# Hybrid attention block: sparse keys and values loaded in two halves, two silus moved behind the first query tiles, and the output projection's operands split two steps ahead

## The chip, the cores and the metric

The kernel runs on one core of a Trainium2 chip. The core has TensorE (PE in the profile) for matrix products, VectorE (DVE), ScalarE (ACT) and GpSimd (POOL) for elementwise work, and a queue (SP) from which most transfers are issued to 16 DMA engines. The metric is the device time of one execution in microseconds (us); smaller is better.

## The reference

One layer of a decoder with three head groups that read the same normalised input, 1024 positions of width 2048, all in float32:

```
h = rmsnorm(x, norm_g) @ w_in                    # one projection feeds everything
o_mla = mla_mixer(...) * silu(z_mla)             # 8 heads, latent attention, dense causal
o_nsa = nsa_mixer(...) * silu(z_nsa)             # 4 heads: compressed + selected + window branches
o_mem = memory_mixer(...) * silu(z_mem)          # 4 heads over 256 memory tokens
out = rmsnorm(x + concat(o_mla, o_nsa, o_mem) @ w_out, final_norm_g)
```

In the sparse (nsa) group each of 8 query tiles of 128 rows attends, per head, to 63 compressed blocks, to the selected keys `k_s, v_s` (here all earlier ones) and to a window of 512 of `k_w, v_w`.

## The kernel before

**Arithmetic.** Each float32 operand is split into a high and a low part (`split`: ACT writes the high part on line 118, DVE subtracts on line 112), and each product is three matmuls (`mm3`, lines 124 to 126). A 128x512 matmul then starts every 0.23 us.

**Buffers.** `big` (16 buffers of 128x2048), `slot` (8 of 128x1088), `wraw` (3) and `work` (4 of 128x1024 each) are pools; a tile waits until a buffer of its pool is free. PSUM has 8 banks: 4 `S`, 2 `T`, 2 `O`/`J`.

**Order.** There are three stages. In the input projection (to 1000 us of the profile) and in the output projection (from 1557 us) the instructions of PE, ACT, DVE and POOL keep the order in which the program writes them (`manual_schedule`); each engine executes its own in order. SP's queue, and everything in the attention stage between them, is ordered by a planner from its own estimates of durations. Every engine's queue, SP's too, is worked off in order: an instruction that waits holds up those behind it.

**Input projection.** Forty units `u` of 7 steps `s` each; a step is a product of 12 matmuls into one `S` bank, and `evac` takes it out. In the second half of the units `evac` adds the first half's sum from DRAM with an accumulating transfer from POOL's queue (lines 782 and 786). `post` finishes a unit; for the last unit it is two silus on ACT (line 795) and their stores, written after the last step. `at(u, s, ...)` hangs other work on a step: in the last unit `ul` the loads of the sparse group. `nsa_keys` loads the keys `ks` (4 `slot` tiles, which also get the compressed keys), `nsa_window` the window's keys (2 `big`), `nsa_aux` the causal mask of the compressed branch (`cmask`, `cm01`) and its values, `nsa_values_in` the values (2 `big`), and `nsa_masks` (line 1063) copies the masks on ACT.

**First query tiles.** For each head `h` and tile `i`, `nsa_scores` fills one to four `S` banks with scores, DVE adds the masks and takes the minimum (lines 1107 to 1114, and 1229 for the compressed branch with `cmask`), ACT takes the exponential (line 659) and so frees the bank, and after the reciprocal the weights are scaled (ACT line 1159, DVE and POOL line 1161), transposed, split and multiplied by the values. Tile `i` reads columns up to `128*(i+1)`, so tiles 0 to 3 need only the first 512 keys.

**Output projection.** 56 steps `t = 8p + k` of 24 matmuls (5.44 us), seven parts `p` of a fast matrix product. Step `t` multiplies the split attention output `ent[t]` (a `slot`) by the split weights `wsp[t]` (a `big`). `w_load`, `a_load` fetch them four steps ahead, `w_prep` splits the weights, `a_prep` first forms sums of attention outputs (part 2, 3 and 5) and then splits. After the last step of a part `oevac` takes all 8 banks out (lines 1612 to 1622). Beside it `oside` adds the residual, squares rows (line 1575), and in part 6 computes `inverse` (the row's 1/rms) and `scaled_out` of rows 0 to 3, on DVE (line 1595) or, with `on_act`, on ACT (line 1593). The last four steps' operands (52 to 55) are multiplied bank by bank at the end.

Of the kernel before, what the change touches and what calls it, by code (L numbers as in the profile page):

```python
# [52 lines left out]
def hybrid_block_kernel(ctx: ExitStack, tc, a, out):  # L53
# [734 lines left out]
    def post(u, n):  # L788
        p, uu = divmod(u, NU)
        o, j = outs[u][n], units[uu][n]  # L790
        if not p:
            V.tensor_tensor(o, o, mst["Rx"], op=ALU.mult)
            store(c0d[uu][:, n * 1024:(n + 1) * 1024], o)
        elif j >= T_ZMLA:
            S.activation(o, o, AF.Silu)
            store(zd[j - T_ZMLA], o)
        elif j < 8:
            store(cd[j], o)
            c_sum(j, o)
# [206 lines left out]
    at(ul, 0, lambda: nsa_keys())  # L1006
    at(ul, 1, lambda: nsa_window())
    at(ul, 3, lambda: nsa_aux())
    at(ul, 4, lambda: nsa_values_in())
    at(ul, 6, lambda: nsa_masks())  # L1010
# [13 lines left out]
    def nsa_window():  # L1024
        kw = big()
        nsa["kwm"] = (kw[:, :1024], kw[:, 1024:])
        load(f(kw), kwd)
        kw = big()
        kw1, kw2 = nsa["kw"] = kw[:, :1024], kw[:, 1024:]
        for r0 in (0, 64):  # L1030
            load(f(kw1[r0:r0 + 64]), kswh[64:])
        load(f(kw2[:64]), kswl[64:])
        load(f(kw2[64:]), posd[:, 64:])

    def nsa_values_in():
        nsa["vs"], nsa["vw"] = big(), big()
        load(f(nsa["vs"]), vsd)
        load(f(nsa["vw"]), vwd)

    def nsa_keys():  # L1040

        kh, kl, k1, k2 = [slot() for _ in range(4)]
        nsa["ks"] = (kh, kl), k1, k2
        load(f(kh[:, :64]), kcd[:, :64])
        load(f(kl[:, :64]), kcd[:, 64:128])
        load(f(k1[:, :64]), kcd[:, 128:192])
        load(f(k2[:64, :64]), kcd[:64, 192:])
        load(f(kh[:, 64:]), ksd[:, :1024])
        load(f(kl[:, 64:]), ksd[:, 1024:])
        for r0 in (0, 64):  # L1050
            load(f(k1[r0:r0 + 64, 64:]), kswh[:64])
        load(f(k2[:64, 64:]), kswl[:64])
        load(f(k2[64:]), posd)
# [26 lines left out]
    post(2 * NU - 1, 0)  # L1080
    post(2 * NU - 1, 1)
# [326 lines left out]
    for h in range(4):  # L1408
        q = qn
        for i in range(8):  # L1410
# [5 lines left out]
            src = nsa_scores(h, q, i)  # L1416
            if h == 3 and i == 7:
# [69 lines left out]
    def a_prep(t, dst=None):  # L1487
# [8 lines left out]
        if p == 2:  # L1496
            V.tensor_tensor(s1, r[0], r[1], op=ALU.add)
            V.tensor_tensor(s2, s1, r[2], op=ALU.subtract)
            src = s2
        elif p == 3:  # L1500
            V.tensor_tensor(r[0], r[0], r[1], op=ALU.subtract)
            src = r[0]
        elif p == 4:
            src = s1
        elif p == 5:
            V.tensor_tensor(s2, r[0], s2, op=ALU.subtract)
            src = s2
        else:
            src = r[0]
        e = slot()[:, :1024] if dst is None else dst  # L1510
        split(e[:, :512], e[:, 512:], src)
        ent[t] = e

    def o_first():

        e = big()
        for t in range(2):
# [3 lines left out]
            a_prep(t, e[:, t * 1024:t * 1024 + 1024])  # L1521
# [111 lines left out]
    def oside(p, k):  # L1633

        i = k // 2
        if p == 1 and k % 2 == 0:
            Y[i] = big(F32)
            load(Y[i][:, L_], a["x"][i * P:(i + 1) * P, L_])
        if p == 3 and k < 4:
# [12 lines left out]
        if p == 6:  # L1652
            if k < 4:
                square(Y[k][:, L_], st_(k, 0))
                square(Y[k][:, H_], st_(k, 1))
            if 0 < k <= 4:
                r = inverse(k - 1, 2)
                scaled_out(k - 1, r, L_)
# [6 lines left out]
    w_prep(2)  # L1665
    a_prep(2)
    for t in range(NT):
        p, k = divmod(t, 8)
        if t + 4 < NT:
            w_load(t + 4)  # L1670
            a_load(t + 4)
        if t + 3 < NT:
            w_prep(t + 3)
            a_prep(t + 3)
# [141 lines left out]
```

## Time and profile before

| | |
|---|---|
| median of 3 runs | 1892.62 us (1887.09 to 1897.51) |
| profiled execution | 1892.9 us, span 1891.1 us |
| PE busy | 1786.8 us (94% of the span) |
| DVE, ACT, POOL busy | 1317.0, 854.9, 323.8 us |
| DMA | 351.91 MB, mean 186 GB/s |
| mean granted clock of TensorE | 0.979 |

A row of the timeline gives start, duration, engine, line, operation, out<-in, shapes and, in brackets, the engine's idle time just before and what ended it. The granted clock is a share of full speed: 1.00 is 2.4 GHz, 0.50 is 1.2 GHz.

### The profile page before, as it was taken

The numbers are of one execution on the slowest core, as the hardware profiler recorded it, in microseconds if no ns is written. First come the engines' busy times: TensorE is split into PE (matmuls) and PEld (weight loads), VectorE is DVE, ScalarE is ACT, GpSimd is POOL, SyncE is SP. The second block draws the span as 40 slices with busy tenths as digits, with TensorE's granted clock in tenths as the row PEclk, the third lists the DMA queues.
The fourth block names the chain that finished last, engine by engine and source line by source line (L and its number), as shares of the span: only waits on it lengthen the run. The fifth ranks groups of instructions, "written<-read, shape, count | busy, mean of one in ns | idle before, by whom it ended". The sixth has DMA issues, their size and how long they took to land. (4 is left out here: it accounts for less than half of the span.)

```text
span 1891.1 us, 26430 instructions
## 1 busy us (share of the span) xinstructions
PE 1786.8 (94%) x9294; PEld 1523.0 (81%) x9294; DVE 1317.0 (70%) x2478; ACT 854.9 (45%) x1712; POOL 323.8 (17%) x433
## 2 busy tenths in 40 slices
PE   8999999999999999999997999999999999989996
PEld 7888878887777777877776898888998988877885
DVE  7976878976866655666564887868778783454777
ACT  8754222222434344544555665545455453222344
POOL 0002322323233313233231222200000000000020
PEclk9999999999999999999998999999999999999998
DMA  6554877786678657978998233432122144654564
GB/s 220 187 189 165 286 263 267 253 298 237 225 211 255 161 173 231 293 214 243 307 265 242 68 97 109 167 114 62 46 77 64 57 154 150 226 167 145 172 194 191
DMA packets 124930, 351.91 MB, mean 186 GB/s; under 512 B 15355, under 2 KB 39613, under 8 KB 121725
## 3 DMA queue, kind: packets, MB, share of 16 engines
q1 hardware_dynamic: 119037, 329.25, 51.7%
q0 software_dynamic: 5760, 20.97, 6.3%
q8 instruction: 73, 1.20, 0.3%
q14 instruction: 60, 0.49, 0.1%
HBM read 242.14 MB, written 108.02 MB: 185 GB/s over the span
## 5 line engine op out<-in xcount | busy, mean ns | idle before, releaser
L124 PE MATMUL S<-big,wh 128*128 128x512 f32 x1336 | 528.7, 396 | 25.2 <-DVE work L772 8.3
L125 PE MATMUL S<-big,wh 128*128 128x512 f32 x1336 | 525.7, 393 | 4.4 <-DVE big L112 4.4
L126 PE MATMUL S<-big,wh 128*128 128x512 f32 x1336 | 525.3, 393 | 1.3 <-DVE wh L112 1.2
L124 PEld LDWEIGHTS S<-big,wh 128*128 128x128 f32 x1336 | 254.0, 190 | 82.0 <-issue 12.5
L125 PEld LDWEIGHTS S<-big,wh 128*128 128x128 f32 x1336 | 254.3, 190 | 56.7 <-DVE big L112 5.9
L126 PEld LDWEIGHTS S<-big,wh 128*128 128x128 f32 x1336 | 253.6, 190 | 56.9 <-DVE wh L112 3.0
L112 DVE TENSOR_TENSOR wh<-wraw,wh 128x512 fp32r<-128x512 f32 (+2 forms) x226 | 199.0, 882 | 73.8 <-ACT wh L118 73.6
L118 ACT ACTIVATE wh<-wraw 128x512 fp32r<-128x512 f32 (+2 forms) x226 | 145.4, 659 | 90.4 <-PE S L126 44.2
L112 DVE TENSOR_TENSOR big<-wraw,big 128x1024 fp32r<-128x1024 f32 x56 | 73.9, 1320 | 105.1 <-ACT big L118 100.5
L733 POOL TENSOR_TENSOR wraw<-wraw 128x512 f32<-128x512 f32 x38 | 56.6, 1488 | 459.6 <-DMA wraw<-in_w_feat 394.6
L659 ACT ACTIVATE work<-S,st 128x512 f32<-128x512 f32 (+3 forms) x148 | 84.6, 573 | 86.5 <-DVE st L1114 35.1
L118 ACT ACTIVATE wh<-rs 128x512 fp32r<-128x512 f32 x80 | 50.2, 628 | 157.7 <-POOL rs L734 125.6
L112 DVE TENSOR_TENSOR wh<-rs,wh 128x512 fp32r<-128x512 f32 x80 | 63.0, 787 | 65.5 <-ACT wh L118 65.4
L118 ACT ACTIVATE big<-wraw 128x1024 fp32r<-128x1024 f32 x56 | 59.2, 1056 | 85.6 <-PE J L126 59.4
L124 PE MATMUL J<-big,wh 128*128 128x512 f32 x214 | 84.1, 393 | 0.8 <-ACT wh L118 0.7
L125 PE MATMUL J<-big,wh 128*128 128x512 f32 x214 | 84.0, 393 | 0.0
L126 PE MATMUL J<-big,wh 128*128 128x512 f32 x214 | 83.9, 392 | 0.0
L118 ACT ACTIVATE wh<-T 128x512 fp32r<-128x512 f32 (+2 forms) x112 | 53.0, 504 | 45.6 <-PE T L1179 29.5
L770 ACT ACTIVATE work<-S 128x512 f32<-128x512 f32 x40 | 23.9, 597 | 106.7 <-PE S L126 99.2
L112 DVE TENSOR_TENSOR wh<-T,wh 128x512 fp32r<-128x512 f32 (+2 forms) x112 | 61.5, 569 | 10.6 <-ACT wh L118 10.3
L1443 POOL MEMSET wh<- 128x128 f32 x64 | 13.8, 228 | 291.8 <-PE O L125 173.6
L1096 PE MATMUL S<-big,big 128*128 128x512 f32 (+2 forms) x144 | 52.9, 367 | 9.7 <-ACT wraw L659 9.7
(378 smaller groups left out, 4132.1 us busy)
## 6 DMA issues: line engine op xcount, KB each, us to landing
wraw<-in_w_feat SPq DMA_DIRECT2D x80, 512.0 KB, 5.5
part<-work SPq DMA_DIRECT2D x40, 512.0 KB, 3.7
work<-part POOLq DMA_DIRECT2D x40, 512.0 KB, 6.4
work<-og SPq DMA_DIRECT2D x72, 256.0 KB, 4.0
wh<-in_w_o SPq DMA_DIRECT2D x32, 512.0 KB, 7.2
t<-wh SPq DMA_DIRECT2D x32, 512.0 KB, 3.0
wraw<-t SPq DMA_DIRECT2D x32, 512.0 KB, 3.7
wraw<-in_w_o SPq DMA_DIRECT2D x24, 512.0 KB, 3.9
```

Source lines behind the costliest of these rows:

```text
L112: V.tensor_tensor(dst, src, f(hi), op=ALU.subtract)
L118: S.activation(hi, src, AF.Copy)
L124: PE.matmul(dst, sh, mh, start=start, stop=False, skip_group_check=shared)
L125: PE.matmul(dst, sh, ml, start=False, stop=False, skip_group_check=shared)
L126: PE.matmul(dst, sl, mh, start=False, stop=stop, skip_group_check=shared)
L659: S.activation(dst, src, AF.Exp, bias=m, scale=-1.0, accum_out=s)
L733: E.tensor_tensor(B12, B22, B12, op=ALU.subtract)
L770: S.activation(C21, B, AF.Copy)
L1096: PE.matmul(d, qm[0][:, c:c + P], km[0][:, k0:k0 + n], start=True, stop=False)
L1443: G.memset(f(t[:, o:o + P]), 0.0)
```

## The change

It has four pieces. (1) The keys, window keys and values of the sparse group are loaded in two halves of 512 columns; the first halves of keys and values and the masks' copy are written one step earlier than before, the masks' load three steps, the window's first half where it was; the second halves follow at step 5 of the last unit. (2) The two last silus move out of the input projection: they are written behind `nsa_scores` of tiles 1 and 2 of the first head, and kept behind the ACT instruction that the program wrote before them. (3) In the output projection `a_prep` becomes `a_sum`, still three steps ahead, and `a_split`; the splits of weights and attention outputs are written two steps ahead instead of three. (4) Rows 0 to 3: the squares of the lower half move from part 6 to part 2, where POOL also multiplies that half by the final gain; its scaling in part 6 goes to ACT instead of DVE.

```
-    def post(u, n):
+    def post(u, n, pin=False):
...
-            S.activation(o, o, AF.Silu)
+            x = S.activation(o, o, AF.Silu)
+            if pin:
+                tc.keep_in_program_order(x)
...
-    at(ul, 0, lambda: nsa_keys())
-    at(ul, 1, lambda: nsa_window())
-    at(ul, 3, lambda: nsa_aux())
-    at(ul, 4, lambda: nsa_values_in())
-    at(ul, 6, lambda: nsa_masks())
+    at(ul - 1, 6, lambda: nsa_keys(0))
+    at(ul, 0, lambda: nsa_aux())
+    at(ul, 1, lambda: nsa_window(0))
+    at(ul, 3, lambda: nsa_values_in(0))
+    at(ul, 5, lambda: nsa_masks(), lambda: nsa_keys(1), lambda: nsa_window(1), lambda: nsa_values_in(1))
...
+    def nsa_values_in(n):
+        if n == 0:
+            nsa["vs"], nsa["vw"] = big(), big()
+        c = slice(512 * n, 512 * n + 512)
+        load(halves(f(nsa["vs"]))[:, :, c], halves(vsd)[:, :, c])
+        load(halves(f(nsa["vw"]))[:, :, c], halves(vwd)[:, :, c])
...
-    post(2 * NU - 1, 0)
-    post(2 * NU - 1, 1)
...
             src = nsa_scores(h, q, i)
+            if h == 0 and i in (1, 2):
+                post(2 * NU - 1, i - 1, True)
...
-    def a_prep(t, dst=None):
+    def a_sum(t):
...
+    def a_split(t, dst=None):
         e = slot()[:, :1024] if dst is None else dst
-        split(e[:, :512], e[:, 512:], src)
+        split(e[:, :512], e[:, 512:], asrc.pop(t))
...
+        if p == 2 and k < 4:
+            square(Y[k][:, L_], st_(k, 0))
+            G.tensor_tensor(Y[k][:, L_], Y[k][:, L_], gf[:, L_], op=ALU.mult)
...
         if p == 6:
             if k < 4:
-                square(Y[k][:, L_], st_(k, 0))
                 square(Y[k][:, H_], st_(k, 1))
...
-                scaled_out(k - 1, r, L_)
+                scaled_out(k - 1, r, L_, True)
...
-    w_prep(2)
-    a_prep(2)
+    a_sum(2)
     for t in range(NT):
...
+        if t + 2 < NT:
+            w_prep(t + 2)
+            a_split(t + 2)
         if t + 3 < NT:
-            w_prep(t + 3)
-            a_prep(t + 3)
+            a_sum(t + 3)
```

`nsa_keys` and `nsa_window` are cut in the same way, each of their transfers into two of 512 columns.

## Rows read from the trace of the kernel before

**Rows 1.** Waits of PE over the whole span: total us, times, longest.

```profile
PE S L1096 <- ACT wraw L659: 16.3, 7, 9.7
...
PE S L124 <- DVE big L1616: 5.1, 1, 5.1
PE S L124 <- DVE big L1622: 4.0, 1, 4.0
```

**Rows 2.** Timeline of ACT from the end of the input projection to the fourth tile.

```profile
1011.63 0.68 ACT L1063 ACTIVATE rs<-wraw 128x576 fp32r<-128x576 f32 x1 [5.15 <-DMA wraw<-in_cm]
1012.33 1.28 ACT L795 ACT_TABLE_LOAD   x1
1013.63 2.00 ACT L795 ACTIVATE work<-work 128x1024 f32<-128x1024 f32 x2
1015.65 1.28 ACT L659 ACT_TABLE_LOAD   x1
...
1024.42 0.29 ACT L659 ACTIVATE wraw<-S,st 128x64 f32<-128x64 f32 x1
```

**Rows 3.** Timeline of PE there: the end of its longest wait.

```profile
1018.15 0.69 PE L1096 MATMUL S<-big,big 128*128 128x384 f32 x1 [9.67 <-ACT wraw L659]
```

**Rows 4.** Timelines there: DVE's last evacuation and POOL's last accumulating transfer.

```profile
1000.28 0.69 DVE L784 TENSOR_TENSOR work<-work,S 128x512 f32<-128x512 f32 x1 [2.03 <-PE S L126]
...
1001.27 0.86 POOL L786 DMA_DIRECT2D work<-part  x1 [1.63 <-DVE work L784]
```

**Rows 5.** Transfers issued from 970 to 1020 us: count, size, median us to landing.

```profile
work<-part POOLq DMA_DIRECT2D x4, 512.0 KB, 8.9
...
wraw<-in_cm SPq DMA_DIRECT2D x1, 32.0 KB, 14.7
```

**Rows 6.** Busy time by stretch: PE (and instructions), PEld, DVE, ACT, POOL, clock, DMA, GB/s.

```profile
1020.00:1025.00 5.00, 5.00 (x24) 4.65 (x24) 3.15 (x11) 3.58 (x11) 1.47 (x6) 0.60 0.27 102
...
1690.00:1700.00 10.00, 9.44 (x30) 7.59 (x31) 4.60 (x8) 0.90 (x1) 0.00 (x0) 0.68 0.22 80
1700.00:1710.00 10.00, 10.00 (x46) 8.29 (x45) 5.04 (x6) 2.51 (x5) 0.00 (x0) 1.00 0.54 160
...
1740.00:1750.00 10.00, 8.88 (x33) 7.27 (x34) 5.77 (x10) 1.58 (x2) 0.00 (x0) 0.83 0.18 52
```

**Rows 7.** Timeline at the end of part 2 (all engines).

```profile
1685.52 1.06 ACT L118 ACTIVATE big<-wraw 128x1024 fp32r<-128x1024 f32 x1 [1.85 <-DMA wraw<-t]
...
1689.73 2.48 DVE L1616 TENSOR_TENSOR big<-big,S 128x512 f32<-128x512 f32 x4
...
1690.56 0.77 PE L124 MATMUL S<-big,wh 128*128 128x512 f32 x1 [5.13 <-DVE big L1616]
```

**Rows 8.** Timelines of DVE, ACT and PE in part 6 and after it.

```profile
1835.92 2.59 DVE L112 TENSOR_TENSOR big<-wraw,big 128x1024 fp32r<-128x1024 f32 x1 [2.22 <-ACT big L118]
...
1852.67 1.22 DVE L112 TENSOR_TENSOR big<-wraw,big 128x1024 fp32r<-128x1024 f32 x1
1853.80 0.69 DVE L112 TENSOR_TENSOR wh<-work,wh 128x512 fp32r<-128x512 f32 x1
1854.41 0.15 DVE L1580 TENSOR_REDUCE st<-st 128x1 f32<-128x2 f32 x1
...
1855.98 2.48 DVE L1595 SCALAR_TENSOR_TENSOR big<-big,st,big 128x1024 f32<-128x1024 f32 x2
1858.38 1.22 DVE L112 TENSOR_TENSOR big<-wraw,big 128x1024 fp32r<-128x1024 f32 x1
...
1854.88 1.04 ACT L118 ACTIVATE big<-wraw 128x1024 fp32r<-128x1024 f32 x1
...
1868.29 1.16 ACT L1593 ACTIVATE big<-big,st 128x1024 f32<-128x1024 f32 x1 [1.06 <-DVE st L1587]
...
1859.65 0.80 PE L125 MATMUL S<-big,wh 128*128 128x512 f32 x1 [2.60 <-DVE big L112]
```

**Rows 9.** POOL's gain product in part 5, and SP in part 3.

```profile
1835.01 2.41 POOL L1651 TENSOR_TENSOR big<-big,big 128x1024 f32<-128x1024 f32 x1 [11.78 <-ACT work L1575]
...
1719.76 0.80 SPq L102 DMA_DIRECT2D work<-og  x2
```

More of the change, by code (lines that the diff above doesn't have):

```diff
@@ L1022, in nsa_q @@
         return (q[:, :1024], q[:, 1024:]), q1, q2
[L1024 to L1029, printed above, removed]
-        for r0 in (0, 64):
[L1031 to L1049, printed above, removed]
+    def halves(t):
+        return t.rearrange("p (t c) -> p t c", t=2)
+    def nsa_window(n):
+        if n == 0:
+            nsa["w"] = big(), big()
+        km, kr_ = nsa["w"]
+        nsa["kwm"] = (km[:, :1024], km[:, 1024:])
+        kw1, kw2 = nsa["kw"] = kr_[:, :1024], kr_[:, 1024:]
+        c = slice(512 * n, 512 * n + 512)
+        load(halves(f(km))[:, :, c], halves(kwd)[:, :, c])
+        for r0 in (0, 64):
+            load(f(kw1[r0:r0 + 64, c]), kswh[64:, c])
+        load(f(kw2[:64, c]), kswl[64:, c])
+        load(f(kw2[64:, c]), posd[:, 64 + 512 * n:576 + 512 * n])
@@ new lines, in nsa_values_in, with nsa_keys @@
+    def nsa_values_in(n):
+        if n == 0:
+            nsa["vs"], nsa["vw"] = big(), big()
+        c = slice(512 * n, 512 * n + 512)
+        load(halves(f(nsa["vs"]))[:, :, c], halves(vsd)[:, :, c])
+        load(halves(f(nsa["vw"]))[:, :, c], halves(vwd)[:, :, c])
+    def nsa_keys(n):
+        if n == 0:
+            kh, kl, k1, k2 = [slot() for _ in range(4)]
+            nsa["ks"] = (kh, kl), k1, k2
+            load(f(kh[:, :64]), kcd[:, :64])
+            load(f(kl[:, :64]), kcd[:, 64:128])
+            load(f(k1[:, :64]), kcd[:, 128:192])
+            load(f(k2[:64, :64]), kcd[:64, 192:])
+            load(f(k2[64:, :64]), posd[:, :64])
+        (kh, kl), k1, k2 = nsa["ks"]
+        c, d = slice(512 * n, 512 * n + 512), slice(64 + 512 * n, 576 + 512 * n)
+        load(f(kh[:, d]), ksd[:, c])
+        load(f(kl[:, d]), ksd[:, 1024 + 512 * n:1536 + 512 * n])
@@ L1050, in nsa_keys @@
         for r0 in (0, 64):
-            load(f(k1[r0:r0 + 64, 64:]), kswh[:64])
-        load(f(k2[:64, 64:]), kswl[:64])
-        load(f(k2[64:]), posd)
+            load(f(k1[r0:r0 + 64, d]), kswh[:64, c])
+        load(f(k2[:64, d]), kswl[:64, c])
+        load(f(k2[64:, d]), posd[:, d])
     def nsa_aux():
@@ L1485, in a_load @@
         araw[t] = places
-    def a_prep(t, dst=None):
+    asrc = {}
+    def a_sum(t):
         p, k = divmod(t, 8)
@@ L1498, in a_prep @@
             V.tensor_tensor(s2, s1, r[2], op=ALU.subtract)
-            src = s2
+            asrc[t] = s2
         elif p == 3:
             V.tensor_tensor(r[0], r[0], r[1], op=ALU.subtract)
-            src = r[0]
+            asrc[t] = r[0]
         elif p == 4:
-            src = s1
+            asrc[t] = s1
         elif p == 5:
             V.tensor_tensor(s2, r[0], s2, op=ALU.subtract)
-            src = s2
+            asrc[t] = s2
         else:
-            src = r[0]
+            asrc[t] = r[0]
+    def a_split(t, dst=None):
         e = slot()[:, :1024] if dst is None else dst
-        split(e[:, :512], e[:, 512:], src)
+        split(e[:, :512], e[:, 512:], asrc.pop(t))
         ent[t] = e
@@ L1520, in o_first @@
             w_prep(t)
-            a_prep(t, e[:, t * 1024:t * 1024 + 1024])
+            a_sum(t)
+            a_split(t, e[:, t * 1024:t * 1024 + 1024])
     d, own = lat_pieces(0, None)
```

## Prediction

> **What bounds the kernel now.** PE does, almost everywhere: it is busy for 94% of the span. So I read where it waits first, then the stretches around those waits, then what the other engines do in them. In the waits of PE [rows 1] the reader is to see that one kind leads, scores waiting for an exponential on ACT, 16.3 us with 9.7 in one piece; two single waits of 5.1 and 4.0 us stand out in the output projection. The change touches just these three places, and a fourth, part 6.
>
> *The seam between input projection and attention.* The 9.7 us wait ends at 1018.15 [rows 3]. ACT shows why [rows 2]: it copies the masks only at 1011.63, released by the transfer of `cm01`, which took 14.7 us to land [rows 5]. Behind the copy in ACT's order stand a table load, the two silus and another table load; the exponentials, which free the score banks that PE waits for, come after 1016.9. The chain is: masks late, ACT held, banks held, PE idle. After it PE runs at a granted clock of 0.50 at first: the mean is 0.60 from 1020 to 1025 [rows 6].
>
> *End of part 2.* PE stops after step 23 and waits 5.13 us for `oevac` [rows 7]. DVE's order has the weight split for step 26 ahead of the evacuation. That split needs a `big` buffer, and here 13 of 16 are taken (8 result rows, the gain, 4 sums), so three are left for weights: the split for `t+3` must wait until PE has finished `t`. ACT starts it at 1685.52, and DVE's evacuation begins at 1689.73. The row names a transfer as releaser; I take the buffer to be the cause, since the start falls just behind the last matmul of the step. The end of part 3 is the same with 4.02 us [rows 1]. After both the granted clock is low for a while (0.68 and 0.83 over 10 us) [rows 6].
>
> *Part 6.* PE waits for the split weights of steps 54 and 55 (the last such wait is 2.60 us, ending at 1859.65); DVE's split for 55 begins at 1858.38 [rows 8]. DVE's chain sets this, one `inverse` and two scalings per step, 5.71 us from the split at 1852.67 to that at 1858.38.
>
> **The change, part by part.**
>
> *Masks, keys, halves: the seam's wait goes.* The masks' load is written three steps earlier and with only the keys' first halves ahead of it instead of all keys and the window. I expect it to land before step 5 of the last unit, so that the copy costs ACT 0.7 us under PE's last steps. The number of transfers grows by 14; SP is not on the path, and the bytes are the same. Tiles 0 to 3 read first halves only, and the second halves have until tile 4, over 10 us behind the start. The keys take 4 of 8 `slot` buffers one step earlier; three or four weight splits remain alive beside them, as before, so I cost that at nothing; if one split came late, its step would slip by about 1 us (row 1852.67 is such a split, 1.22 us).
>
> What is late next is the ramp of ACT. DVE is free at 1000.97 [rows 4], so tile 0's minimum is there at about 1001.4. From the second table load at 1015.65 to tile 3's first exponential at 1024.42 ACT needed 8.8 us [rows 2]; plus one exponential done before the stall (0.6), the same work from 1001.4 ends at 1010.8. That is 13.6 us earlier, the upper bound.
>
> *Silus behind tiles 1 and 2.* Each is 1.00 us (2.00 for two) with a load of its table and one back, 1.28 each: 3.56 us, so 7.1 for both apart, 4.6 if no exponential falls between them; before, both stood in the stall. Behind them on ACT wait the exponentials of the next tiles, behind those PE. Fully exposed they leave 13.6 - 7.1 = 6.5 us; below that lies the case of the transfer: the silu's input comes by the accumulating transfer of 1001.27 [rows 4], whose kind took 8.9 us to land [rows 5], so it is there at 1010.2, and if ACT reaches the silu sooner, it holds the exponentials as the masks did. Then about 2 us are left of the gain. I take 13.6 - 4.6 = 9.0 us, because PE has the transposes of tiles 0 and 1 and two score groups to do meanwhile, and keep 2 and 13.6 as bounds.
>
> The row of the second table load ends at 1013.61 and the silu starts at 1013.63 [rows 2]: a switch costs the load and nothing visible else. The Trainium skill ("ScalarE: Activation LUTs", section "What ACT_TABLE_LOAD costs") counts a drain of 1.38 us more per switch, and advises to group functions by table, which this change undoes; by it the four switches would cost an estimated 5.5 us more, and the gain here would be 3.5 instead of 9.0. The trace does not show that drain.
>
> *Splits two steps ahead.* Now the split for `t+2` waits for PE's step `t-1`, not `t`: it runs at the start of step `t` and takes about 4 us (ACT 1.04, DVE 1.22 and 0.69, a sum 0.69) [rows 8] of the step's 5.44. The evacuation then starts before the step ends; as the banks finish one after another through the last step, PE finds bank 0 free when the next part starts. So both stalls go: 5.13 and 4.02 us [rows 1]. With them goes the slow stretch. From 1690.56 to 1700 PE made 30 matmuls, and at 46 per 10 us they need 6.5 of those 9.4 us: 2.9 lost. After 4.02 us of waiting, 8.9 us of the stretch from 1740 hold 33, which need 7.2: 1.7 lost [rows 6]. Together 13.75 us. Bounds: 9.1 if the slow stretches came from elsewhere, and nothing if the evacuation still met a late split. The other ends of parts have no such stall now and get none: there more buffers are free. The attention sums (`a_sum`) keep their lead, and their `work` buffers come free when they did, since the split's true start is the same end of a step of PE.
>
> *Squares and gain in part 2.* Four squares (1.1 us each on ACT) and four POOL products of 2.41 us [rows 9]. A DVE split beside such a product took 2.59 instead of 1.22 us [rows 8]: 1.4 us more in each of steps 16 to 19, on top of 3.3 us, still under 5.44. Cost nothing; PE's cover is two steps of prepared operands.
>
> *Part 6: a loss.* After `oevac` of part 5 DVE used to have the split for 51 next (1835.92), then 52, and three rounds of `inverse` and scaling up to 55. Now the split for 50 stands in that place, so five intervals lie before 55 instead of four. A round becomes: weight split 1.13, attention split 0.61, `inverse` 1.57 (starts of 1852.67 to 1855.98), the scaling on ACT 1.16, and ACT's next high part 0.96 before DVE can go on: 5.43 instead of 5.71 [rows 8]. From 1835.92 to 1858.38 are 22.5 us; plus one round 5.4, less 0.8 for three shorter rounds and 1.1 for a square that no longer stands ahead: 26.0, so step 55's weights come 3.6 us later. PE waits for them in its first bank, so the end moves by 3.6. Bounds: 0, if ACT's scaling hides, and 6, with a longer slow stretch.
>
> **Sum**, against the profiled execution's 1892.9 us (span 1891.1; the median of the runs is 1892.62): 1892.9 - 9.0 - 13.75 + 3.6 = 1873.75, so 1873.5 on the median's scale.
>
> **Rivals.**
>
> *The seam gives little.* The silus wait on ACT for the accumulated sums and hold the exponentials. For: 8.9 us to landing, and the second halves are queued beside them. Against: the silus stand behind the scaling of tiles 1 and 2, some 6 us later than tile 0's scores. Gain 2: 1880.5 us.
>
> *The drain of the table rule is there.* A stop behind each table switch; against it stands the 0.02 us between load and silu. 5.5 us more: 1879 us.
>
> *The stalls at the ends of parts 2 and 3 stay*, that is, the edit does not do what it says, because the transfer named in [rows 7] and not the buffer was the cause. Then -9.0 + 3.6: 1887.5 us. Against: splits in that part start with the end of a step of PE.
>
> *Slower: `work` runs dry in part 3.* Four buffers serve the attention loads of steps 28 to 31 and four residual loads that are kept until part 4. SP issued step 31's load only at 1719.76 [rows 9], in step 28, and its sum now stands a step earlier in DVE's order. If DVE waits there, and SP's weight loads queue behind the residual's, each step concerned loses up to 5.44 us. It decides once four steps are lost (3.5 x 5.44 = 19); at five the time is 1901 us. Against: the load lands some 3 us later, within the slack of two steps.
>
> **How the numbers follow.** Forecast 0.72 (its own range 1867 to 1881); little at the seam 0.13; drain 0.03; stalls stay 0.05; slower 0.04; 0.03 for a planner's new order of the attention stage that costs over 10 us. A measurement here can tell about 0.5%, 9.5 us, so faster means below 1883.2: forecast, seam and drain less a little for their tails, 0.86; same 0.09; slower 0.05. The low end is the upper bound at the seam and no loss in part 6, rounded in: 1866. The high end takes in the seam case with a worse part 6: 1884.
>
> **What would show it.** Right: the masks' copy before 1000 us, no wait of PE over 4 us between 1000 and 1030, tile 3's exponential near 1012 to 1016, no wait for lines 1616 and 1622, and clock 1.00 behind both ends; in part 6 a longer wait of PE than before. Wrong: a long idle of ACT ahead of a silu, PE waiting on splits within parts 2 or 3, or heads 2 to 4 of the sparse group taking longer than before.

## Result: 1872.4 us, 1.1% faster, and the profile after

The changed kernel's median is 1872.4 us (5 runs, 1871.04 to 1877.05) against 1892.62 us before (5 runs, 1887.09 to 1897.51). The ratio is 0.9892, 95% interval 0.987 to 0.9915. Its profiled execution took 1871.04 us, span 1869.3 us. The forecast was 1873.5.

The totals hide where the time went, so I cut both profiled executions at points that both have: the first score of the sparse group, the last minimum of its compressed branch, and the evacuation of the last bank (`J`) of each part of the output projection. The table gives the microseconds between them. The later kernels are in it too; each is described below.

| kernel | median | first score at | scores to last minimum | to end of part 1 | parts 2 and 3 | rest to last `J` |
|---|---|---|---|---|---|---|
| before | 1892.62 | 1000.08 | 213.60 | 428.27 | 102.53 | 136.95 |
| changed | 1872.40 | 1000.50 | 204.99 | 425.80 | 88.67 | 139.72 |
| e1 output projection only | 1881.22 | 1002.11 | 212.68 | 429.00 | 88.66 | 139.62 |
| e2 seam only | 1882.18 | 1003.13 | 207.27 | 426.08 | 101.87 | 136.87 |
| e3 gain late | 1875.77 | 1001.56 | 213.08 | 425.57 | 88.67 | 136.49 |
| e4 evacuation first | 1875.39 | 995.32 | 214.95 | 426.04 | 88.67 | 137.03 |
| e5 lead regained | 1865.90 | 1001.12 | 205.05 | 425.58 | 88.67 | 133.42 |
| e6 silus "together" | 1877.94 | 1003.38 | 208.91 | 428.12 | 88.67 | 139.79 |
| e7 silus in front | 1881.07 | 1000.46 | 213.34 | 428.34 | 88.67 | 139.87 |
| e8 whole loads | 1877.15 | 996.23 | 210.18 | 425.56 | 88.67 | 139.62 |
| e9 silus only | 1897.20 | 1002.43 | 218.05 | 425.95 | 102.41 | 136.84 |
| e10 silus later | 1868.78 | 1000.33 | 212.13 | 428.38 | 88.67 | 131.83 |
| e11 gain late, all | 1872.69 | 997.98 | 205.17 | 426.12 | 88.70 | 140.29 |

How to read it: the last `J` of the changed kernel came 21.75 us earlier (1859.68 instead of 1881.43), and that is +0.42 (first score), -8.61 (seam and sparse heads), -2.47 (latent attention, part 1), -13.86 (parts 2 and 3) and +2.77 (rest). The whole of the -8.61 stands in the first head: from the first score to the last minimum of that head are 39.79 us instead of 48.36, and the three heads behind it take 165.2 us in both. Medians alone would be a poor guide to parts of this size: the first score lies anywhere from 995.3 to 1003.4 in these profiled executions.

At the seam, the timeline of ACT in the changed kernel answers to [rows 2]:

```profile
993.11 0.69 ACT L1077 ACTIVATE rs<-wraw 128x576 fp32r<-128x576 f32 x1 [0.28 <-DMA wraw<-in_cm]
993.81 1.28 ACT L659 ACT_TABLE_LOAD   x1
1001.74 0.32 ACT L659 ACTIVATE wraw<-S,st 128x64 f32<-128x64 f32 x1 [6.64 <-DVE st L1241]
...
1008.06 1.28 ACT L795 ACT_TABLE_LOAD   x1
1009.35 1.06 ACT L795 ACTIVATE work<-work 128x1024 f32<-128x1024 f32 x1
...
1010.80 1.28 ACT L659 ACT_TABLE_LOAD   x1
...
1014.70 1.28 ACT L795 ACT_TABLE_LOAD   x1
1016.00 1.06 ACT L795 ACTIVATE work<-work 128x1024 f32<-128x1024 f32 x1
1017.07 1.28 ACT L659 ACT_TABLE_LOAD   x1
1018.37 0.31 ACT L659 ACTIVATE wraw<-S,st 128x64 f32<-128x64 f32 x1
```

The masks' copy is at 993.11 instead of 1011.63, the first exponential follows its minimum, and the silus (line 795) stand among the exponentials without a wait of their own. Tile 3's exponential is at 1018.37 instead of 1024.42. PE's longest wait there fell from 9.67 us [rows 3] to 2.75, as its timeline shows:

```profile
1012.83 0.59 PE L1108 MATMUL S<-wh,big 128*128 128x448 f32 x1 [2.75 <-ACT wraw L659]
```

At the end of part 2, timelines of ACT and DVE against [rows 7]: the last high part of weights that precedes the evacuation starts at 1669.42, 38.13 us behind the last `J` of part 1, where [rows 7] have 43.57: a whole step earlier. The evacuation (line 1635) begins while PE is still in the step's last banks, and not 4 us after its end.

```profile
1669.42 1.06 ACT L118 ACTIVATE big<-wraw 128x1024 fp32r<-128x1024 f32 x1 [3.86 <-issue]
...
1672.86 2.47 DVE L1635 TENSOR_TENSOR big<-big,S 128x512 f32<-128x512 f32 x4
```

PE has no wait for an evacuation left. The view by stretch (columns as in [rows 6]) has first the seam, then the 10 us behind the ends of parts 2 and 3, which lie at 1674 and 1718 here: PE is full at clock 1.00 where it had been at 0.68 and 0.83 [rows 6]. The last two rows show the price in part 6:

```profile
1010.00:1015.00 5.00, 2.25 (x8) 1.81 (x8) 3.01 (x9) 4.31 (x9) 0.83 (x3) 0.80 0.96 240
1015.00:1020.00 5.00, 3.74 (x26) 3.50 (x25) 0.88 (x4) 4.96 (x10) 0.00 (x0) 0.86 0.96 340
1020.00:1025.00 5.00, 3.43 (x22) 2.63 (x21) 4.36 (x12) 3.43 (x11) 1.71 (x8) 1.00 0.79 284
...
1674.00:1684.00 10.00, 10.00 (x46) 8.29 (x45) 8.49 (x13) 3.16 (x4) 0.00 (x0) 1.00 0.57 190
1718.00:1728.00 10.00, 10.00 (x46) 8.29 (x45) 8.65 (x12) 4.43 (x6) 0.00 (x0) 1.00 0.36 113
...
1830.00:1840.00 10.00, 5.17 (x10) 2.82 (x11) 6.64 (x13) 4.30 (x7) 0.00 (x0) 0.61 0.53 211
1840.00:1850.00 10.00, 10.00 (x41) 8.12 (x40) 4.36 (x11) 3.59 (x9) 0.00 (x0) 0.88 0.16 62
```

Part 6 itself, timelines of DVE and PE against [rows 8]:

```profile
1810.55 2.58 DVE L112 TENSOR_TENSOR big<-wraw,big 128x1024 fp32r<-128x1024 f32 x1 [2.22 <-ACT big L118]
...
1830.65 1.23 DVE L112 TENSOR_TENSOR big<-wraw,big 128x1024 fp32r<-128x1024 f32 x1 [0.90 <-ACT big L118]
...
1836.15 1.23 DVE L112 TENSOR_TENSOR big<-wraw,big 128x1024 fp32r<-128x1024 f32 x1 [0.90 <-ACT big L118]
...
1831.19 0.50 PE L124 MATMUL S<-big,wh 128*128 128x512 f32 x1 [2.73 <-ACT wh L118]
1836.69 0.80 PE L124 MATMUL S<-big,wh 128*128 128x512 f32 x1 [3.37 <-ACT wh L118]
```

Five intervals, the last three of 5.5 us each, lie between the split of step 50 (1810.55) and that of step 55 (1836.15): 25.60 us where 22.46 us lay before between the splits of 51 and 55. The wait is longer than the 2.60 us of before, as forecast; the rows name the high part of the attention output, which ACT makes, and not the weights, as what PE waited for.

The marks of the table are DVE's evacuations, and one of them misleads. PE's last product on bank `J` in part 5 and the evacuation of that bank, by the timelines of PE and DVE, first before, then changed:

```profile
1829.46 0.39 PE L126 MATMUL J<-big,wh 128*128 128x512 f32 x1
1830.76 0.67 DVE L1620 TENSOR_TENSOR big<-big,J 128x512 f32<-128x512 f32 x1
```

```profile
1804.94 0.39 PE L126 MATMUL J<-big,wh 128*128 128x512 f32 x1
1805.37 0.69 DVE L1639 TENSOR_TENSOR big<-big,J 128x512 f32<-128x512 f32 x1
```

The evacuation was 1.30 us behind PE before and is 0.43 now. PE itself needs 43.52 us for part 5 in every kernel here. So part 6 is counted below from PE's last product on `J` in part 5 to that in part 6: 51.55 us before, 54.31 in the changed kernel, 2.76 more, which is the +2.77 of the table.

### The profile page after: what moved, and what is told of

Same layout as the page of the kernel before. It is cut to its first block, busy times and chain, and to the rows that moved or that the text cites. A ratio compares the mean times of both kernels' runs of the same rounds, so it can differ in the third digit from the quotient of the medians.

```text
span 1869.3 us, 26472 instructions
## 1 busy us (share of the span) xinstructions
PE 1780.7 (95%) x9294; PEld 1516.8 (81%) x9294; DVE 1317.5 (70%) x2474; ACT 861.7 (46%) x1718; POOL 332.8 (18%) x437
## 4 chain that ended last, share of the span: by engine, by line
PE 43%; DVE 5%; ACT 4%; issue 2%; DMA 2%; POOL 1%; SPq 0%; POOLq 0%; ACTq 0%; DVEq 0%
PE S L124 4%; PE S L125 4%; PE S L126 4%; PE J L124 3%; PE J L125 3%; PE J L126 3%; PE O L125 3%; PE O L124 2%; PE O L126 2%; PE T L1191 2%; PE S L1108 1%; PE S L1109 1%; PE S L1111 1%; PE S L1112 1%; PE S L1110 1%
## 5 line engine op out<-in xcount | busy, mean ns | idle before, releaser
L112 DVE TENSOR_TENSOR big<-wraw,big 128x1024 fp32r<-128x1024 f32 x56 | 78.2, 1396 | 91.6 <-ACT big L118 89.8
L1191 PE MATMUL T<-ident,work 128*128 128x128 f32 x383 | 58.9, 274 | 2.1 <-DVE wh L112 1.4
```

Source lines behind the costliest of these rows:

```text
L112: V.tensor_tensor(dst, src, f(hi), op=ALU.subtract)
L1191: PE.transpose(T[:, t * P:t * P + P], blocks[i + t][1], ident)
```

## The experiments

### Each half of the change alone

**e1** takes the kernel before and only the output projection of the change. (All ratios are to the kernel before, run beside each group of experiments; its medians there were 1892.2 to 1894.1 us.)

```diff
...
+        if t + 2 < NT:
+            w_prep(t + 2)
+            a_split(t + 2)
         if t + 3 < NT:
-            w_prep(t + 3)
-            a_prep(t + 3)
+            a_sum(t + 3)
```

> The kernel before, with only the output projection changed (splits two steps ahead, squares and gain in part 2, scaling on ACT); the seam is as before. My theory: the two places add up, so this alone is worth the 13.75 us of the two ends less 3.6 us in part 6: about 10 us below the kernel before, some 1882 us. The evacuation of part 2 ends about 7 to 8 us earlier against the end of part 1, that of part 3 another 6, no wait of PE for an evacuation, granted clock 1.00 behind both ends, and the step before last in part 6 is 3.6 us later. Rival, that the transfer of the raw weights and not the buffer held the split: both waits stay, gain 0 or a loss of 3.6. Rival on the unforecast 2.5 us at the end of the latent attention: if the changed output projection moved them (its first loads and splits run there), they come here too, and the first transposed matmul of the output projection is 2.5 us earlier than in the kernel before.

Median 1881.22, ratio 0.9929 (0.991 to 0.9948). Parts 2 and 3 take 88.66 us, 13.87 less than before; the rest is 2.67 us longer. PE's wait at the seam is still there, by its timeline:

```profile
1019.88 0.69 PE L1096 MATMUL S<-big,big 128*128 128x384 f32 x1 [8.72 <-ACT wraw L659]
```

The 2.5 us at the end of the latent attention did not come (429.00); in e2, below, they did (426.08).

**e2** takes only the loads and silus of the seam; the output projection is that of the kernel before.

```diff
-    at(ul, 0, lambda: nsa_keys())
...
-    at(ul, 6, lambda: nsa_masks())
+    at(ul - 1, 6, lambda: nsa_keys(0))
...
+    at(ul, 5, lambda: nsa_masks(), lambda: nsa_keys(1), lambda: nsa_window(1), lambda: nsa_values_in(1))
...
+            if h == 0 and i in (1, 2):
+                post(2 * NU - 1, i - 1, True)
```

> The kernel before, with only the seam changed (keys and values in halves, masks earlier, silus behind the first query tiles); the output projection is as before. My theory: 8 us at the seam, so about 1884 us; both waits at the ends of parts 2 and 3 stay at about 5.1 and 4.0 us, part 6 as before. The 2.5 us at the end of the latent attention come here if they follow from the attention stage lying otherwise against something of fixed place (about 10.7 us at the start of the output projection and 1882 us), and don't come if they hang on the output projection's edit. Rival that the seam gains nothing in itself and only shifts waits: 1892.

Median 1882.18, ratio 0.9934 (0.9912 to 0.9955). The seam is worth 6.3 us here, against 8 expected and 8.6 in the changed kernel; 1.1 of the difference lies in the third head, where this execution's clock was 0.78 and 0.88 from 1090 to 1100 us and the changed kernel's 1.00. The two waits stand where they stood. Waits of PE from part 2 on (total, times, longest):

```profile
PE S L124 <- DVE big L1630: 5.1, 1, 5.1
PE S L124 <- DVE big L1636: 3.7, 1, 3.7
```

So the halves act in different places, and neither stands in for the other.

### What held the evacuation at the ends of parts 2 and 3

**e3** keeps lead and order of the kernel before and only gives parts 2 and 3 one more `big` buffer, by taking the gain's late:

```diff
-    gf = big(F32)
-    load(gf, a["fg"])
+    gf_ = []
...
+        if t == 36:
+            gf_.append(big(F32))
+            load(gf_[0], a["fg"])
```

> The kernel before, unchanged in lead and order, but the gain's buffer of the output projection is taken and loaded only in step 36 instead of before step 0, so that in parts 2 and 3 four buffers instead of three are left for split weights. Theory buffer: the split three steps ahead no longer waits for the end of a step of PE, both waits of 5.1 and 4.0 us go with their low clock, and the time falls by 9 to 14 us, to 1879 to 1884. Rival transfer: the raw weights land too late whatever buffers there are; the split still starts at the end of the step, both waits stay, 1892 within 2 us.

Median 1875.77, ratio 0.9898 (0.9875 to 0.9922). ACT's timeline shows the high part for step 26 at 1678.34:

```profile
1678.34 1.06 ACT L118 ACTIVATE big<-wraw 128x1024 fp32r<-128x1024 f32 x1 [1.86 <-DMA wraw<-t]
```

Counted from the end of part 1 (last `J` at 1640.21 here, 1641.95 before), that is 38.13 us instead of 43.57 [rows 7]: one step earlier. Parts 2 and 3 take 88.67 us. The row still names a transfer of raw weights as releaser, as [rows 7] did, with those transfers untouched and the wait of PE gone. The trace of before speaks against that name too: the raw weights' transfers issued at 1671.54, 1676.98 and 1682.42 took 3.6, 4.4 and 3.7 us, so none landed between 1681.4 and 1686.1, and the high part started at 1685.52. The buffer was the cause.

**e4** keeps buffers and lead, and in two steps writes the evacuation ahead of the split:

```diff
+        late = t in (23, 31)
-        if t + 3 < NT:
+        if t + 3 < NT and not late:
             w_prep(t + 3)
             a_prep(t + 3)
...
+        if late:
+            w_prep(t + 3)
+            a_prep(t + 3)
```

> The kernel before with its lead of three steps, but in steps 23 and 31 alone the split for three steps ahead is written behind the evacuation instead of ahead of it. My theory, that the evacuation stood behind the late split in DVE's order: both waits of PE (5.1 and 4.0 us) go, 9 to 14 us, so 1879 to 1884 us; the split that is now later has two steps of cover. Rival, that the evacuation is itself short of something at the end of a part (DVE busy, the banks): the waits stay or move into the next part, within 3 us of 1892.

Median 1875.39, ratio 0.9901 (0.9881 to 0.9921), and again 88.67 us for the two parts. DVE's timeline shows the evacuation and the split that it was behind before:

```profile
1678.66 2.48 DVE L1616 TENSOR_TENSOR big<-big,S 128x512 f32<-128x512 f32 x4
...
1683.45 1.22 DVE L112 TENSOR_TENSOR big<-wraw,big 128x1024 fp32r<-128x1024 f32 x1
```

PE has no wait behind the later split: what is prepared covers it. Three cures, a shorter lead, one buffer, or the order of two pieces, end at the same 88.67 us: PE is full there and nothing more is to be had. The medians of e3 and e4 fell by more than this place gives (about 18 us against 13.9). In e4's profiled execution the remainder lies ahead of part 2: the first score is 4.76 us earlier and the latent attention with part 1 is 2.23 us shorter, against 1.35 us lost at the seam. The edit touches nothing there.

### The price in part 6

**e5** is the changed kernel, with the lead of three steps taken up again before part 6:

```diff
+    prepped = 1
...
-        if t + 2 < NT:
-            w_prep(t + 2)
-            a_split(t + 2)
-        if t + 3 < NT:
+        if t >= 44 and t + 3 < NT:
+            a_sum(t + 3)
+        while prepped < min(t + (2 if t < 44 else 3), NT - 1):
+            prepped += 1
+            w_prep(prepped)
+            a_split(prepped)
+        if t < 44:
             a_sum(t + 3)
```

> The changed kernel, but from step 44 on the splits run three steps ahead again (steps 46 and 47 are both split at step 44; in part 6 the order of the kernel before). My theory of part 6: the loss there, 3.64 us from the last evacuation of part 5 to the end, is one round of inverse and scaling that fell ahead of the split for step 55; with the lead back it goes, so part 6 takes 50 to 51 us instead of 54.3 and the waits of PE for split weights (2.7 and 3.4 us) shrink to some 1 to 2.6 us; about 3 us faster than the changed kernel on any run. Rival: the loss comes from scaling on ACT, which also makes the high parts of the weights; then part 6 stays at 54 us. Part 2 and 3 unchanged at 88.7 us together.

Median 1865.9 (1864.17 to 1873.41), ratio 0.9866 (0.9836 to 0.9896). Part 6 takes 48.01 us; it was 54.31 in the changed kernel and 51.55 before. Waits of PE from the end of part 1 on, the whole list:

```profile
PE S L124 <- ACT wh L118: 1.7, 1, 1.7
PE S L125 <- DVE big L112: 0.2, 1, 0.2
```

In the changed kernel they were 6.1 us in two. So the lead of two steps costs 6.30 us, and the squares moved to part 2 and the scaling on ACT give 3.54 us back (51.55 less 48.01); the change's +2.76 in this part is the difference. I had expected 50 to 51 us and 3 us of gain; the loss is twice that. That the scaling on ACT made it is refuted. Of the 6.3 us, 4.4 are waits (6.3 us in all against 1.9); the rest fits the clock behind them, which was 0.61 and 0.88 from 1830 to 1850 in the changed kernel and 0.83 and 1.00 in e5. e10 below has the output projection of e5 and the same two waits, 1.72 and 0.24 us, but there the clock stayed at 1.00, and part 6 took 46.42 us. So the price of the lead is 6.3 to 7.9 us and what the rest gives back 3.5 to 5.1.

### What held the exponentials at the seam

**e7** puts the two silus back ahead of the attention and leaves the changed loads.

```diff
+    post(2 * NU - 1, 0)
+    post(2 * NU - 1, 1)
     assert not side, side.keys()
...
-            if h == 0 and i in (1, 2):
-                post(2 * NU - 1, i - 1, True)
```

> The changed kernel, but the two silus stand ahead of the attention again as in the kernel before; masks, keys and halves as changed. My theory: the masks were what came last, and the silus behind the tiles add to it: with the silus in front ACT does 2.56 us of table loads and 2 us of silus, and waits for their input, ahead of the first exponential, so the stretch from the start of the sparse scores to the end of part 1 is 4 to 8 us longer than in the changed kernel. Rival: the silus cost the same wherever they stand, then 0 within 1 us, and the masks alone are the gain.

The whole gain of the seam is gone: 213.34 us, 8.35 more than in the changed kernel; the four kernels with the old seam have 212.7 to 215.0. ACT's timeline:

```profile
1008.42 1.28 ACT L795 ACT_TABLE_LOAD   x1 [6.32 <-DMA work<-part]
1009.71 1.06 ACT L795 ACTIVATE work<-work 128x1024 f32<-128x1024 f32 x1
1012.05 1.06 ACT L795 ACTIVATE work<-work 128x1024 f32<-128x1024 f32 x1 [1.28 <-DMA work<-part]
```

The masks are early here, and now the accumulating transfers hold ACT: their sums are there at 1008.42 and 1012.05.

**e9** does the other half, the silus behind tiles 1 and 2 with the loads of the kernel before.

```diff
...
-    post(2 * NU - 1, 0)
-    post(2 * NU - 1, 1)
...
+            if h == 0 and i in (1, 2):
+                post(2 * NU - 1, i - 1, True)
```

> The kernel before, with only the two silus moved behind the query tiles 1 and 2; keys, window, values and masks are loaded whole and in the old order. With the silus in front and early masks the seam gained nothing, so two things stand in ACT's way one behind the other. My theory: each edit alone brings nothing, since the masks land at about 11 us behind the start of the sparse scores and the silus' inputs at about 9 to 12 us; here the masks hold ACT, the wait of PE stays at 8 to 10 us, and the stretch from the start of the scores to the end of part 1 is 638 to 642 us as in the kernel before, or up to 3 us longer for the second pair of table loads. Rival: the silus' place alone makes the gain and the masks do not matter; then 631 to 633 us.

Median 1897.2, ratio 1.0019 (1.0003 to 1.0036); the seam takes 218.05 us, 4.4 more than before. Timelines of ACT and PE: the masks hold the exponentials. PE's wait there is 5.84 us and not the expected 8 to 10; two more, of 2.24 and 2.11 us, follow at the exponentials behind the silus, which now have four table loads instead of two.

```profile
1014.57 0.68 ACT L1065 ACTIVATE rs<-wraw 128x576 fp32r<-128x576 f32 x1 [4.92 <-DMA wraw<-in_cm]
...
1016.82 0.69 PE L1096 MATMUL S<-big,big 128*128 128x384 f32 x1 [5.84 <-ACT wraw L659]
```

So ACT stood behind two waits that ended at almost the same time: the masks at 1011.63 in the kernel before, the second silu's input at 1012.05 in e7. In the kernel before itself the transfer for that input was issued at 1001.27 [rows 4] and landed 10.1 us later, at 1011.4. Removing the one uncovers the other; the change removes both.

**e6** was to put both silus behind tile 2.

```diff
-            if h == 0 and i in (1, 2):
-                post(2 * NU - 1, i - 1, True)
+            if h == 0 and i == 2:
+                post(2 * NU - 1, 0, True)
+                post(2 * NU - 1, 1)
```

> The changed kernel, but both silus stand behind tile 2 of the first head, one table switch to and fro instead of two. My theory: the silus on ACT lie about half in PE's way; one pair of table loads less, 2.56 us, is worth 1 to 2.6 us at the seam (from the start of the sparse scores to the end of part 1). Rival: they are hidden anyway, 0. Rival, the drain rule of the Trainium skill (ScalarE: Activation LUTs, section What ACT_TABLE_LOAD costs): each switch costs 1.38 us more than its load, then up to 5.3 us.

The edit did not make the experiment: the second silu, which was not kept in program order, was put by the planner ahead of the first, and they stayed apart with two pairs of table loads. So it says nothing on the price of a switch. It shows the margin instead. The silu that came first reads the later of the two transfers, and ACT's timeline shows what that does:

```profile
1008.03 1.28 ACT L795 ACT_TABLE_LOAD   x1
1014.23 1.06 ACT L795 ACTIVATE work<-work 128x1024 f32<-128x1024 f32 x1 [4.92 <-DMA work<-part]
```

ACT waits 4.92 us, and the stage is 3.9 us longer than in the changed kernel.

**e8** loads keys, window and values whole, at the places of the first halves; all slices become the whole width.

```diff
-    at(ul, 5, lambda: nsa_masks(), lambda: nsa_keys(1), lambda: nsa_window(1), lambda: nsa_values_in(1))
+    at(ul, 5, lambda: nsa_masks())
...
-        c = slice(512 * n, 512 * n + 512)
+        c = slice(0, 1024)
```

> The changed kernel, but keys, window and values are loaded whole at the places of the first halves (same order, same bytes, 14 transfers fewer); masks at the same place behind them. My theory: the order alone brings most of it, but the masks and values land some microseconds later since all bytes stand ahead of them: the masks' copy 5 to 10 us later than in the changed kernel and part of the 8.5 to 11 us lost again, 2 to 6 us. Rival, halves cost nothing and bring nothing: masks land in time all the same, no difference within 1 us. Rival, the smaller transfers of the halves cost descriptors and bandwidth: faster than the changed kernel by 1 to 2 us.

210.18 us, 5.2 more than the changed kernel, though the total can't tell (median 1877.15, 1871.39 to 1882.93). The timelines of ACT and PE show the masks' copy 3.7 us ahead of the first score (7.4 in the changed kernel), still in time, and PE waiting for the last keys of the window:

```profile
992.52 0.69 ACT L1077 ACTIVATE rs<-wraw 128x576 fp32r<-128x576 f32 x1 [3.96 <-DMA wraw<-in_cm]
...
1000.25 0.47 PE L1112 MATMUL S<-big,big 128*128 128x256 f32 x2 [1.57 <-DMA big<-pos]
```

Of the 5.2 us, 4.0 lie in the first head and 1.1 in the third, where this execution's clock was 0.85 and 0.81 from 1085 to 1095 us and the changed kernel's 1.00. So the halves are worth some 4 us in this execution. The masks, which I had expected to be late, were in time; the one transfer that PE waits for is that of the window's keys. That wait is 1.57 us, and ACT's first silu comes 12.1 us behind the first score instead of 8.9. I put the loss down to those keys; how 1.57 us become 4 is not shown, and no run tests it.

**e10** is e5 with the silus one tile later; the lines that e5 adds are left out here.

```diff
-            if h == 0 and i in (1, 2):
-                post(2 * NU - 1, i - 1, True)
+            if h == 0 and i in (2, 3):
+                post(2 * NU - 1, i - 2, True)
```

> The changed kernel with the lead of three steps regained from step 44 on, and the silus one tile later, behind tiles 2 and 3. If the silus still stand in PE's way while ACT fills the first banks, a tile more of cover helps: the first long wait of PE (2.75 us) shrinks and the stretch to the end of part 1 is 1 to 3 us shorter than 630.7. Rival: each silu holds one of the four work buffers and the planner's order behind it; one tile more makes tile 2 or 3 wait for a buffer and it is equal or up to 4 us longer.

The profiled execution has 212.13 us at the seam, 7.1 more than e5. ACT's timeline has the largest piece:

```profile
1009.27 0.47 ACT L659 ACTIVATE work<-S,st 128x256 f32<-128x256 f32 x1 [4.78 <-DMA z<-work]
```

An exponential into a `work` buffer waits for the store of an earlier result (`z` from `work`) to free it. PE's wait behind it is 4.18 us; 1.1 us more lie in the third head, again at a lower clock. The timed runs were less hard hit: the profiled one is the slowest of four (1872.66, median 1868.78), and by the ratios to the kernel before, 0.9865 (0.9837 to 0.9894) against 0.9866, e10 and e5 can't be told apart. So whether one tile later is worse is open. In the profiled execution the place behind tiles 1 and 2 lies between the sums' landing on one side and the four `work` buffers on the other.

### The lead kept throughout

**e11** is e2 with the gain's buffer taken in step 36 as in e3, the squares in part 2, the four products with the gain in part 5 on POOL, and the scaling on ACT.

```diff
...
+        if p == 2 and k < 4:
+            square(Y[k][:, L_], st_(k, 0))
+        if p == 5 and k % 2 == 0:
+            G.tensor_tensor(Y[i][:, L_], Y[i][:, L_], gf_[0][:, L_], op=ALU.mult)
```

> The seam as in the changed kernel, the lead of three steps kept throughout, the gain's buffer taken only in step 36 (so that a fourth buffer is there for split weights in parts 2 and 3), the four squares of the first rows in part 2, their products with the gain in part 5 on POOL, and their scaling on ACT. Theory, that only the lack of a buffer ever made two steps of lead better: parts 2 and 3 together 88.7 us, part 5 43.5 to 44.4, part 6 about 48 us, total as the changed kernel with the lead regained, about 1866 us, 6 us below the changed kernel. Rival: four more POOL products in part 5 beside DVE slow its scaling chain and part 5 or 6 is 2 to 4 us longer.

Median 1872.69. Parts 2 and 3 are at 88.70 us, as expected. Counted by DVE's evacuations part 6 is at 47.43 and part 5 at 50.97 instead of 43.5; PE is in time through part 5 and then waits, and its part 6 is 54.88 us instead of about 48. Timelines of POOL, DVE and PE:

```profile
1770.68 2.39 POOL L1668 TENSOR_TENSOR big<-big,big 128x1024 f32<-128x1024 f32 x1 [25.16 <-ACT work L1588]
1773.03 3.38 POOL L1655 TENSOR_TENSOR big<-big,big 128x1024 f32<-128x1024 f32 x1
...
1771.59 2.57 DVE L112 TENSOR_TENSOR big<-wraw,big 128x1024 fp32r<-128x1024 f32 x1 [2.17 <-ACT big L118]
1774.08 2.88 DVE L1520 TENSOR_TENSOR big<-work,big 128x512 f32<-128x512 f32 x1
...
1807.46 0.76 PE L124 MATMUL S<-big,wh 128*128 128x512 f32 x1 [4.12 <-DVE big L1633]
```

Beside two POOL products in a row DVE's split takes 2.57 instead of 1.22 us and a sum 2.88 instead of 0.69. The next two pairs of POOL products, from 1785.36 and 1798.71, do the same: 2.58 and 2.60 us for the split, 2.88 and 2.85 for what follows it. DVE falls behind, and the wait for an evacuation that was cured in parts 2 and 3 comes back at the end of part 5 with 4.12 us. The rival held in kind; the loss of 6.9 us against e5 is larger than its 2 to 4.

## Why the prediction was right

Of the signs that it named, the masks' copy before 1000, no wait of PE over 4 us from 1000 to 1030, no wait for the evacuations, the clock of 1.00 behind both ends and a longer wait in part 6 (3.37 us against 2.60) came; tile 3's exponential at 1012 to 1016 did not. Of the signs of being wrong none came.

**The sum.** Its three terms, -9.0, -13.75 and +3.6, make -19.15; in the same places the profiled executions have -8.61, -13.86 and +2.77, together -19.70. The medians differ by 20.2 us and the profiled executions by 21.9. What the profiled ones have beyond the three terms, above all -2.47 in the latent attention and part 1, is not the edit's, as shown below; that the medians agree with the forecast to 1.1 us is in part luck.

**Ends of parts 2 and 3: right in cause and size.** Forecast -13.75, measured -13.86. e3 shows the buffer, e4 the order, e1 that it comes from this half of the change. The rival that a transfer held the split fell with e3.

**The seam: right in size, with two errors that cancel.** Forecast -9.0; this pair of executions gives -8.61, and the mean of the four kernels with the old seam (before, e1, e3, e4: 213.58) less that of the four with the new one (changed, e2, e5, e11: 205.62) gives 8.0. The step that was mis-sized is "I take 13.6 - 4.6 = 9.0 us, because PE has the transposes of tiles 0 and 1 and two score groups to do meanwhile". ACT paid the silus in full: between 1008.06 and 1018.37 it spent 7.24 us on four table loads and two silus. Tile 3's exponential came at 1018.37 and not at 1012 to 1016. Counted from the first score that is 6.47 us earlier than before, the prediction's own figure for silus fully exposed (6.5). Against it stands the clock, which I had not counted here. By stretch, before:

```profile
1005.00:1010.00 5.00, 1.95 (x5) 1.24 (x5) 0.00 (x0) 1.47 (x3) 0.00 (x0) 0.69 1.07 235
...
1015.00:1020.00 5.00, 1.59 (x4) 1.09 (x5) 2.38 (x14) 4.57 (x15) 0.55 (x2) 0.50 0.99 345
```

Busy time of PE times the missing share of the clock, with the 0.60 from 1020 to 1025 [rows 6], makes an estimated 3.4 us lost before; the changed kernel's rows above, 0.80 and 0.86 from 1010 to 1020, make 1.0. The 2.4 us between them and the 6.47 us come near the 8.6; that these two make it up is argued from the rows, not tested apart.

**The rival "the seam gives little" was nearer than 0.13 said.** Its mechanism, silus that wait for the accumulated sums and hold the exponentials, is what e6 and e7 show, with 3.9 and 8.4 us lost. In the changed kernel the transfer that adds the first sum was issued at 999.18 and landed 8.4 us later, at 1007.6; ACT begins the table load for its silu at 1008.06 and the silu at 1009.35. That is a margin of half a microsecond ahead of the load and under 2 us ahead of the silu.

**The drain of the table rule.** The Trainium skill ("ScalarE: Activation LUTs", section "What ACT_TABLE_LOAD costs") has 1.38 us more per switch. No run here shows it, and the measurement decides: silus follow their loads by 0.01 to 0.02 us (1008.06 + 1.28 to 1009.35), and the exponential follows its load in the same way (1017.07 + 1.28 to 1018.37).

**Part 6: right in cause, too large in size.** Forecast +3.6, measured +2.76. The terms of the forecast add up to 3.5 (26.0 less 22.5). The forecast of a round, 5.43 us, came out at 5.5, and the five intervals took 25.60 us instead of 26.0. The sum also left the start of the chain where it was: the first split begins 5.61 us behind PE's last product on `J` in part 5 (1810.55 after 1804.94) and began 6.46 us behind it before (1835.92 after 1829.46). Counted so, step 55's split is 2.3 us later and not 3.6. e5 shows that it was the lead, and that the forecast netted a loss of 6.3 us or more against a gain of 3.5 or more.

**`work` running dry in part 3** did not come: PE has no wait there, and the two parts take 88.67 us.

**Not forecast: -2.47 us between the last minimum and the end of part 1.** This stretch has two groups of values, 425.6 to 426.1 and 428.1 to 429.0. Before, e1, e6, e7 and e10 are in the upper one, the others in the lower, with the old and the new seam, and the old and the new output projection, in both. So neither half of the edit decides it, nor do they together: in the changed kernel's own variants e6 and e10 the upper value comes back. The granted clock parts them: in all five profiled executions of the upper group it fell for some microseconds within this stretch, in none of the eight of the lower. Before, e6 and e7 have 0.83 from 1540 to 1550 and again from 1550 to 1560; e10 and e1 have their fall elsewhere. By stretch, first before, then e10, then e1, then e4 of the lower group:

```profile
1540.00:1550.00 10.00, 8.59 (x43) 7.19 (x43) 8.88 (x27) 5.19 (x15) 0.00 (x0) 0.83 0.53 161
1550.00:1560.00 10.00, 8.43 (x44) 7.49 (x45) 8.27 (x13) 7.51 (x12) 0.00 (x0) 0.83 0.68 230
```

```profile
1550.00:1560.00 10.00, 9.13 (x40) 8.41 (x41) 7.57 (x12) 6.45 (x9) 0.00 (x0) 0.67 0.74 227
```

```profile
1235.00:1240.00 5.00, 4.30 (x15) 3.11 (x15) 4.04 (x5) 1.45 (x3) 0.00 (x0) 0.69 0.88 308
```

```profile
1540.00:1550.00 10.00, 7.33 (x49) 6.02 (x48) 9.31 (x23) 6.99 (x15) 0.00 (x0) 1.00 0.41 126
1550.00:1560.00 10.00, 10.00 (x54) 8.58 (x53) 8.04 (x11) 6.03 (x8) 0.00 (x0) 1.00 0.96 327
```

The third head of the sparse group is parted in the same way: 45.2 to 45.3 us in the six executions whose clock fell there (e2, e4, e7, e8, e9, e10), 44.1 to 44.2 in the seven at 1.00. Why the clock falls in one execution and not in another stays open: PE's busy time over these 20 us is much the same in before (17.0) and in e4 (17.3).

## What to carry to other kernels

When one wait is named for a stall, ask what on the same engine would have waited anyway and until when: here the masks (1011.63) and the silus' sums (1012.05) ended together, and either edit alone gave nothing or cost time. When an evacuation waits in an engine's order behind a split that lacks a buffer, a buffer, the order of two pieces, or a shorter lead cure it alike; choose the one that takes nothing elsewhere. The shorter lead took 6.3 us or more in part 6, and the two kernels that take the old lead up again for that part alone are the fastest here (e5 and e10, ratios 0.9866 and 0.9865). Before a difference of 1 to 3 us between two profiled executions is put down to an edit, compare the granted clock of that stretch in both.

## What the runs showed of the hardware

A load of ACT's table can start ahead of the wait of the instruction that it serves, and then costs nothing: the load at 993.81 in the changed kernel was done 6.6 us before its exponential could start, that at 1008.03 in e6 4.9 us before its silu. In e7 the load itself came behind the wait of 6.32 us, and its 1.28 us were paid. What decides between the two is open.

The granted clock can fall in one execution and not in another behind waits of the same length: in part 6 of e5 and e10, the same program there, PE waits 1.72 and 0.24 us; behind that the clock was 0.83 from 1830 to 1840 us in e5 and 1.00 in e10, and part 6 took 48.01 and 46.42 us.

POOL and DVE worked one after the other in e11 rather than side by side: the split begun at 1771.59 ended at 1774.16, which is POOL's end (1773.07) and 1.1 us, and the sum begun at 1774.08 ended at 1776.96, POOL's end (1776.41) and 0.6 us, about their own durations. The Trainium skill ("SBUF — State Buffer", section "SBUF: two separate sides") calls the port pair that the two engines share an exclusive lock, held for a whole instruction; these rows agree.
